# W_down of two sequences in one pass of seven block products

## The chip, the cores and the metric

The kernel runs on one core of one Trainium2 chip. The metric is the device time of one execution in microseconds. Three executions of the kernel before took 2009.88, 2016.78 and 2017.57 us; their median, 2016.78, is the time before.

## The reference

One encoder layer is applied to two sequences that share their weights: a prompt of 1024 tokens and a sample of 512, both with 1024 channels, 16 meta tokens put in front. Its mixing part (attention over a neighbourhood, a Fourier branch, gates) isn't touched by the change. What matters is the end of the layer:

```
x = x + mixed @ w_out
a = relu(rmsnorm(x, g_mlp) @ w_up)          # w_up   (1024, 4096)
return x + (a * a) @ w_down                 # w_down (4096, 1024)
```

then a last RMSNorm, and the meta tokens are dropped. Everything is float32. A product of two float32 matrices is made of three matmuls in a faster 32-bit format: each operand is split into a high part (a cast on ACT) and a low part (the operand less its high part, a subtraction on DVE or POOL), and high x high, high x low and low x high are summed (`mm3`, line 116).

## The kernel before

The program is traced in Python and put in order by a planner that works from priorities; each engine and each DMA queue then runs its instructions strictly in its own order. `pinned()` and `behind(marks)` are orders written out by hand: what is traced inside comes, on its own engine, behind the instructions named. Nearly all large transfers are issued on SP's queue. A tile pool with `bufs=n` has n places; an instruction that writes a place waits until its earlier user is done.

The sample comes first, then the prompt.

**The sample's MLP** (class `Mlp`, line 1059). The 4096 hidden channels are 32 slices of 128. `up` makes one slice: the product with W_up (24 matmuls, 512 tokens wide), ReLU on ACT, the square on DVE, and the split into high and low parts, which stay in SBUF. `down` (line 1109) follows for two slices at a time: it loads two slices of W_down, splits them (ACT, then POOL), and for each of the four tiles of 128 tokens and each half of the 1024 columns adds the product onto the tile's sum `acc` on DVE. So up and down alternate, two slices each; the last `down` takes four slices. `combine` (line 1093) makes four combinations T1 to T4 of W_down's blocks on POOL while these lie in SBUF, and stores them in the DRAM tensors `wt`. Between the steps `reading` normalizes and transposes the prompt's rows for the next sequence, and `before_last` loads the prompt's four value weights. At the end the sample's sums are normalized and stored.

**The prompt's MLP** (class `Halves`, line 1161) uses the Strassen-Winograd form: a product of 2 x 2 blocks with seven block products in place of eight. W_up's outputs and their four combinations (`combinations`, line 1471) are stored as eight blocks per pair of slices in `hidden_prompt`. `down` (line 1511) runs the seven products of `DOWN` (line 1485), each a sum over eight units of four slices. A step is one product and one unit: `load` fetches a hidden block and a weight block (512 KB each; b11, b21, b22 come straight from W_down, T1 to T4 from `wt`), splits both three steps ahead, and PE multiplies 24 times, for four tiles of 128 tokens. The results stay in PSUM banks over the eight units, two sets of four banks in turn. `evict` adds a finished product to the sums or to U2 and U3, which several results share. The last product (b22) has its last three units held back and done tile by tile (`apart = 3`), so that the first tiles are normalized (`finish`, line 1543) while PE works on the others. The sums `acc` come back from DRAM during the second and third product.

Of the kernel before, what the change touches and what calls it, by code (L numbers as in the profile page):

```python
# [68 lines left out]
class Layer:  # L69
    def __init__(self, tc, ctx, ins, outs):  # L70
# [17 lines left out]
        self.wt = []  # L88
# [239 lines left out]
    def run(self, order):  # L328
# [3 lines left out]
        for i, (name, T) in enumerate(order):  # L332
# [112 lines left out]
            mlp = self.Mlp(self, hp_, mp, name, T, h2T, acc)  # L445
# [7 lines left out]
            if nxt:  # L453
# [10 lines left out]
            mlp.run(reading, before_last, gate, lambda: tile_("r1").bitcast(F32))  # L464
# [551 lines left out]
    def project_out(self, hp, p, x, T, m, wo, acc, mlp, marks):  # L1016
# [36 lines left out]
        mlp.load(2, self.pair(p, [128, 2, 512], "w", 2))  # L1053
# [5 lines left out]
    class Mlp:  # L1059
        G = 2  # L1060
        NF = FF // 128

        def __init__(self, layer, hp, p, name, T, h2T, acc):
            self.layer, self.nc, self.hp, self.p, self.name, self.T, self.h2T, self.acc = layer, layer.nc, hp, p, name, T, h2T, acc
            self.w, self.hid = {}, {}
            self.ups = [self.up(f) for f in range(self.NF)]

        def load(self, f, to=None):
            if f not in self.w:
                to = to and [x.rearrange("p a (k c) -> p (a k) c", c=128) for x in to]  # L1070
                self.w[f] = self.layer.weights(self.layer.rows("w_up", f * 128), to)

        def up(self, f):
# [4 lines left out]
            hi, lo = (t.rearrange("p a b -> p (a b)") if len(t.shape) == 3 else t  # L1078
                      for t in self.layer.pair(self.hp, [128, T] if T == 512 else [128, 2, 512], "hid", 2 * self.G))
            self.hid[f] = hi, lo  # L1080
            step = 256 if f < 3 and T == 512 else 512
            for c in range(T // step):
# [3 lines left out]
                r = self.p.tile([128, 512], F32, name="relu", bufs=2)[:, :step]  # L1086
                nc.scalar.activation(out=r, in_=ps, func=AF.Relu)  # L1087
                nc.vector.tensor_tensor(out=r, in0=r, in1=r, op=ALU.mult)  # L1088
# [4 lines left out]
        def combine(self, g, even, odd):  # L1093


            nc, wt = self.nc, self.layer.wt
            if g % 2 == 0:
                wt.append(self.layer.dram.tile([128, 2, 4, 512], F32, name=f"wt{g // 2}"))
            (b11, b12), (b21, b22) = ([x[:, i] for i in range(2)] for x in (even, odd))
            t = [self.hp.tile([128, D], F32, name="hn", bufs=2) for _ in range(2)]  # L1100
            t1, t2, t3, t4 = (x[:, i * 512:(i + 1) * 512] for x in t for i in range(2))
            to = [wt[-1][:, g % 2, 2 * i:2 * i + 2].rearrange("p a b -> p (a b)") for i in range(2)]
            for i, ops in enumerate((((t1, b12, b11), (t2, b22, t1)), ((t3, b22, b12), (t4, b21, t2)))):
                for x in ops:
                    nc.gpsimd.tensor_tensor(out=x[0], in0=x[1], in1=x[2], op=ALU.subtract)
                nc.sync.dma_start(to[i], t[i])
                yield

        def down(self, fs, last, gate):

            layer, nc, T, acc, hid = self.layer, self.nc, self.T, self.acc, self.hid
            w, raws = {}, []
            marks = layer.mark()
            for i, f in enumerate(fs):
                to = (layer.pair(self.p, [128, 2, 512], "w", 2 if T == 512 else 4) if i < 2 else
                      tuple(gate()[:, :, :512] for _ in range(2)))
                raw = self.raws[i]().rearrange("p (a b) -> p a b", a=2)
                nc.sync.dma_start(raw, layer.ins["w_down"][f * 128:(f + 1) * 128, :].rearrange("p (a b) -> p a b", a=2))
                w[f] = [t.rearrange("p a b -> p (a b)") if T == 512 else t for t in layer.split_sb(raw, *to)]
                raws.append(raw)  # L1120
            combining = chain(*(self.combine(fs[i] // 2, raws[i], raws[i + 1]) for i in range(0, len(fs), 2)))
            if last:
                for _ in combining:
                    pass
                with layer.behind(marks + layer.mark()):
                    last()
                gain = layer.gain(self.p.tile([128, D], F32, name="gain", bufs=1), "g_final")
            for t in range(T // 128):
                ts = slice(t * 128, (t + 1) * 128)
                for half in range(2):  # L1130
                    cs = slice(half * 512, (half + 1) * 512)
                    ps = layer.psum()
                    layer.mm3(ps, [(hid[f][0][:, ts], hid[f][1][:, ts], *(v[:, cs] if T == 512 else v[:, half] for v in w[f]))
                                   for f in fs])
                    with layer.tc.high_priority(offset=60) if last and t == T // 128 - 1 else nullcontext():
                        nc.vector.tensor_tensor(out=acc[t][:, cs], in0=acc[t][:, cs], in1=ps, op=ALU.add)
                with layer.pinned():
                    next(combining, None)
                if last:
                    o = self.hp.tile([128, D], F32, name="hn", bufs=2)  # L1140
                    with layer.tc.high_priority(offset=60) if t == T // 128 - 1 else nullcontext():
                        layer.norm(acc[t], gain, o, junk=self.p.tile([128, D], BF16, name="junk", bufs=1))
                    nc.sync.dma_start(layer.outs[self.name][t * 128:(t + 1) * 128, :], o)

        def run(self, reading, before_last, gate, raw):
            other = lambda: self.layer.wtile("raw", [128, D]).bitcast(F32)
            self.raws = [raw, lambda: self.p.tile([128, D], F32, name="gain", bufs=1), other, other]
            G, NF = self.G, self.NF
            for g in range(NF // G - 1):
                for f in range(g * G + (G if g else 0), (g + 2) * G):  # L1150
                    for _ in self.ups[f]:
                        pass
                next(reading, None)
                if g < NF // G - 2:
                    self.down(range(g * G, (g + 1) * G), None, gate)
            for _ in reading:
                pass
# [529 lines left out]
```

## Time and profile before

| | us |
|---|---|
| median of three executions | 2016.78 |
| the profiled execution | 2014.83 |
| its span, first to last instruction | 2013.0 |
| PE busy | 1954.8 (97%) |
| POOL busy | 958.6 (48%) |
| DVE busy | 1098.2 (55%) |
| ACT busy | 757.7 (38%) |
| share of the DMA engines on SP's and ACT's hardware queues | 47.6% |
| mean granted TensorE clock | 0.989 |

PE is the engine that does matmuls, PEld its weight loads, which run beside them. Matmuls overlap, so a matmul that is shown with 0.39 us follows its predecessor after some 0.23 us; the distance of starts is what counts. A row of the chain of waits gives the start, the length and the work that the end of the program depended on at that time. A row of the timeline gives the start, the length, the engine and line, and in brackets how long the engine had been idle before it and what ended that. A row of groups gives the number of instructions, the busy time, the mean in ns and the idle time before them; with three durations joined by slashes it gives least, median and greatest. DVE instructions of the same kind differ in length, and their starts can overlap the end of their predecessors by 0.1 us.

### The profile page before, as it was taken

The numbers are of one execution on the slowest core, as the hardware profiler recorded it, in microseconds if no ns is written. First come the engines' busy times: TensorE is split into PE (matmuls) and PEld (weight loads), VectorE is DVE, ScalarE is ACT, GpSimd is POOL, SyncE is SP. The second block draws the span as 40 slices with busy tenths as digits, with TensorE's granted clock in tenths as the row PEclk, the third lists the DMA queues.
The fourth block names the chain that finished last, engine by engine and source line by source line (L and its number), as shares of the span: only waits on it lengthen the run. The fifth ranks groups of instructions, "written<-read, shape, count | busy, mean of one in ns | idle before, by whom it ended". The sixth has DMA issues, their size and how long they took to land.

```text
span 2013.0 us, 26474 instructions
## 1 busy us (share of the span) xinstructions
PE 1954.8 (97%) x9635; PEld 1625.1 (81%) x9635; DVE 1098.2 (55%) x1916; ACT 757.7 (38%) x1325; POOL 958.6 (48%) x743
## 2 busy tenths in 40 slices
PE   6999999999999999999999999999999999999997
PEld 4887787888888878888888888887888888888886
DVE  6572445756666552566663225466666666443246
ACT  3564323433332331556552313224333333433342
POOL 3144535467776740223333223413978774644442
PEclk8999999999999999999999999999999999999999
DMA  6666773354444445455555543412444445976663
GB/s 203 170 161 200 217 228 94 96 178 157 147 156 158 150 154 200 114 139 137 135 180 174 136 118 98 160 63 85 177 168 168 172 154 193 299 236 205 194 193 122
DMA packets 275652, 326.50 MB, mean 162 GB/s; under 512 B 42872, under 2 KB 197240, under 8 KB 274968
## 3 DMA queue, kind: packets, MB, share of 16 engines
q1 hardware_dynamic: 261792, 303.92, 47.6%
q0 software_dynamic: 13728, 20.88, 4.5%
q8 instruction: 76, 1.25, 0.3%
q14 instruction: 56, 0.46, 0.1%
HBM read 235.67 MB, written 91.64 MB: 163 GB/s over the span
## 4 chain that ended last, share of the span: by engine, by line
PE 83%; DVE 6%; DMA 4%; issue 2%; ACT 2%; POOL 2%; SPq 0%; POOLq 0%; DVEq 0%; ACTq 0%
PE ps_mm L128 23%; PE ps_o L128 22%; PE ps_s L128 19%; PE ps_t L128 8%; PE ps_mm L487 2%; PE ps_mm L488 2%; PE ps_mm L489 2%; PE ps_o L629 1%; DMA w_raw<-in_w_in 1%; POOL w_lo L152 1%; PE ps_t L609 1%; DMA bm<-g_un 1%; PE ps_t L193 1%; DMA gain<-in_w_fnB 1%; DVE st L182 1%
## 5 line engine op out<-in xcount | busy, mean ns | idle before, releaser
L152 POOL TENSOR_TENSOR w_lo<-w_raw,w_hi 128x1024 fp32r<-128x1024 f32 x84 | 212.7, 2540 | 210.2 <-ACT w_hi L151 180.3
L151 ACT CAST w_hi<-w_raw 128x1024 fp32r<-128x1024 f32 x100 | 104.7, 1048 | 156.4 <-PE ps_s L128 49.9
L487 PE MATMUL ps_mm<-hT,w_hi 128*128 128x512 f32 (+3 forms) x320 | 126.5, 395 | 0.2 <-DVE k L527 0.2
L1088 DVE TENSOR_TENSOR relu<-relu 128x512 f32<-128x512 f32 (+1 forms) x35 | 63.0, 1801 | 108.0 <-ACT relu L1087 108.0
L488 PE MATMUL ps_mm<-hT,w_hi 128*128 128x512 f32 (+3 forms) x320 | 115.2, 360 | 0.0
L489 PE MATMUL ps_mm<-hT,w_lo 128*128 128x512 f32 (+3 forms) x320 | 115.2, 360 | 0.0
L603 ACT ACTIVATE sc<-sc,ast 128x288 f32<-128x288 f32 (+4 forms) x96 | 53.9, 561 | 76.5 <-DVE ast L601 76.2
L1335 POOL TENSOR_TENSOR x<-w_hi,x 128x512 fp32r<-128x512 f32 (+1 forms) x42 | 69.8, 1662 | 23.0 <-ACT x L1338 23.0
L723 POOL MEMSET bm<- 64x96 f32 (+2 forms) x64 | 11.2, 175 | 144.7 <-DVE ast L601 97.7
L152 POOL TENSOR_TENSOR w_lo<-r,w_hi 128x1024 fp32r<-128x1024 f32 x15 | 36.8, 2452 | 87.5 <-ACT w_hi L151 87.5
L629 PEld LDWEIGHTS ps_o<-pt,vb 104*64 104x64 f32 (+6 forms) x576 | 62.3, 164 | 12.2 <-POOL vb L566 4.7
L152 POOL TENSOR_TENSOR w_lo<-w_hi 128x1024 fp32r<-128x1024 f32 x18 | 45.9, 2550 | 50.0 <-ACT w_hi L151 45.8
L152 POOL TENSOR_TENSOR w_lo<-w_lo,w_hi 128x1024 fp32r<-128x1024 f32 x18 | 48.0, 2668 | 45.2 <-ACT w_hi L151 45.2
L489 PEld LDWEIGHTS ps_mm<-hT,w_lo 128*128 128x128 f32 x320 | 60.4, 189 | 8.6
L629 PE MATMUL ps_o<-pt,vb 104*64 104x128 f32 (+6 forms) x576 | 63.4, 245 | 4.0 <-POOL vb L566 2.1
L566 POOL TENSOR_TENSOR vb<-vr,vb 96x384 fp32r<-96x384 f32 (+4 forms) x48 | 48.7, 1032 | 35.6 <-ACT vb L565 30.5
L128 PE MATMUL ps_t<-gate,x 128*128 128x512 f32 x264 | 65.3, 396 | 0.0
L128 PE MATMUL ps_mm<-gate,x 128*128 128x512 f32 x256 | 64.3, 395 | 0.0
L487 PEld LDWEIGHTS ps_mm<-hT,w_hi 128*128 128x128 f32 x320 | 60.9, 190 | 2.2 <-PE ps_s L597 0.4
L488 PEld LDWEIGHTS ps_mm<-hT,w_hi 128*128 128x128 f32 x320 | 61.0, 191 | 1.7
L601 DVE CUSTOM_DVE_ANT_0 sc<-ps_s,bm 128x288 f32<-128x288 f32 (+4 forms) x96 | 46.3, 482 | 24.4 <-PE ps_s L597 13.7
L152 POOL TENSOR_TENSOR w_lo<-raw,w_hi 128x512 fp32r<-128x512 f32 x24 | 35.5, 1485 | 50.5 <-ACT w_hi L151 42.2
(664 smaller groups left out, 5872.4 us busy)
## 6 DMA issues: line engine op xcount, KB each, us to landing
w_raw<-in_w_in SPq DMA_DIRECT2D x56, 512.0 KB
w_raw<-in_w_up SPq DMA_DIRECT2D x34, 512.0 KB
wt<-hn SPq DMA_DIRECT2D x32, 512.0 KB
hidden_prompt<-h SPq DMA_DIRECT2D x32, 512.0 KB
w_hi<-hidden_prompt SPq DMA_DIRECT2D x20, 512.0 KB
w_raw<-hidden_prompt SPq DMA_DIRECT2D x18, 512.0 KB
w_lo<-hidden_prompt SPq DMA_DIRECT2D x18, 512.0 KB
w_raw<-in_w_out SPq DMA_DIRECT2D x16, 512.0 KB
```

Of the source, the lines that this page charges most:

```text
L128: self.nc.tensor.matmul(out, a, b, start=(i == 0 and not more), stop=(i == len(terms) - 1), skip_group_check=more)
L151: nc.scalar.copy(out=hi, in_=raw)
L152: (lo_engine or nc.gpsimd).tensor_tensor(out=lo, in0=raw, in1=hi.bitcast(F32), op=ALU.subtract)
L487: nc.tensor.matmul(ps, a[0], b[0], start=(kt == 0), stop=False)
L488: nc.tensor.matmul(ps, a[0], b[1], start=False, stop=False)
L489: nc.tensor.matmul(ps, a[1], b[0], start=False, stop=(kt == 7))
L566: nc.gpsimd.tensor_tensor(out=lo, in0=vs, in1=hi.bitcast(F32), op=ALU.subtract)
L601: nc.vector.tensor_tensor_reduce(out=sc[:, :W], in0=ps[:, :W], in1=bm[:, :W], scale=1.0, scalar=3e38, op0=ALU.add, op1=ALU.min, accum_out= ...
L603: nc.scalar.activation(out=sc[:, :W], in_=sc[:, :W], func=AF.Exp, bias=st[:, 0:1], scale=-1.0, accum_out=st[:, 1:2])
L629: nc.tensor.matmul(po[:m, j * 128:(j + 1) * 128], v, x, start=(i == 0), stop=(i == len(ops) - 1))
L1088: nc.vector.tensor_tensor(out=r, in0=r, in1=r, op=ALU.mult)
L1335: self.nc.gpsimd.tensor_tensor(out=to, in0=x, in1=y, op=op)
```

## The change

W_down of the sample is no longer done beside its W_up. The sample's MLP becomes a class `Up` that only makes the hidden slices. It squares them in place and stores them to DRAM as the left factors of the same seven block products, four plain blocks and four combinations made on DVE, per pair of slices. The sums of the sample after `project_out` are stored too (`sums`). Splitting the hidden slices and all loads of W_down go away from this stage, as do the four combinations on POOL and their stores; in their place `Up.combine` makes only T2, for every other unit of four slices, on POOL, and stores it (`t2`).

`Halves.down` then does W_down for both sequences: each step has six tiles instead of four, four of the prompt and two of the sample, with two tiles of `u2` and `u3` more and twelve sums. It loads a prompt block (512 KB), a sample block (256 KB) and the weight blocks. T1, T3 and T4, and T2 of the other units, are no longer loaded but made on DVE from one to four blocks of W_down and T2 (`PARTS`, `parts`) in the raw place of the first; eleven places are shared by these raw blocks, the hidden blocks have two each, and the split operands three instead of four. Products come in another order, and three of them are added on top of the one before in the same banks (`ON_TOP`). Fetch and split both run two steps ahead, the split pinned in order; some sums wait in a list (`late`) and are done one per step, the normalizations of the second half's rows among them. The last two units are held back instead of three.

```diff
-            mlp = self.Mlp(self, hp_, mp, name, T, h2T, acc)
+            self.short = mlp = self.Up(self, ap, hp_, mp, name, T, h2T)
...
-                    for q in range(4):
+                    for q in (2, 3, 0, 1):
...
                 if half:
+                    nc.sync.dma_start(mlp.sums[t], acc[t])
...
+    class Up:
...
+            self.hid = [layer.dram.tile([128, 8, 2, T // 2], F32, name=f"hidden_{name}{u}") for u in range(self.NF // 4)]
+            self.sums = [layer.dram.tile([128, D], F32, name=f"sum_{name}{t}") for t in range(T // 128)]
...
+                if f % 4 > 1 or f >= self.NF - 4:
+                    to = [x.rearrange("p a (k c) -> p (a k) c", c=128) for x in self.layer.pair(self.p, [128, 2, 512], "w", 2)]
...
-                r = self.p.tile([128, 512], F32, name="relu", bufs=2)[:, :step]
-                nc.scalar.activation(out=r, in_=ps, func=AF.Relu)
-                nc.vector.tensor_tensor(out=r, in0=r, in1=r, op=ALU.mult)
-                nc.scalar.copy(out=hi[:, cs], in_=r)
-                nc.vector.tensor_tensor(out=lo[:, cs], in0=r, in1=hi[:, cs].bitcast(F32), op=ALU.subtract)
+                nc.scalar.activation(out=r[:, cs], in_=ps, func=AF.Relu)
+                nc.vector.tensor_tensor(out=r[:, cs], in0=r[:, cs], in1=r[:, cs], op=ALU.mult)
                 yield
...
+            to = self.hid[g // 2][:, :, g % 2]
+            nc.sync.dma_start(to[:, 2 * odd:2 * odd + 2], two(r))
+            if odd:
+                (a11, a21), (a12, a22) = ([two(x)[:, i] for i in range(2)] for x in self.r.pop(g))
...
+                    nc.vector.tensor_tensor(out=k, in0=x, in1=y, op=op)
+                nc.sync.dma_start(to[:, 4:8], sums)
+
+        def combine(self):
...
+                u = g // 2
+                if u % 2:
+                    continue
...
+                nc.sync.dma_start(even, w[g * 256:g * 256 + 128, :])
+                nc.sync.dma_start(odd[:, :512], w[g * 256 + 128:g * 256 + 256, 512:])
                 yield
...
+                nc.gpsimd.tensor_tensor(out=odd[:, :512], in0=odd[:, :512], in1=even[:, 512:], op=ALU.subtract)
+                nc.gpsimd.tensor_tensor(out=odd[:, 512:], in0=odd[:, :512], in1=even[:, :512], op=ALU.add)
+                nc.sync.dma_start(layer.t2[u][:, g % 2], odd[:, 512:])
+                yield
...
-    DOWN = ((0, "b11", 0), (5, "t2", 1), (2, "b21", 0), (6, "t3", 1), (4, "t1", 0), (3, "t4", 1), (7, "b22", 0))
...
+    DOWN = ((0, "b11"), (2, "b21"), (5, "t2"), (6, "t3"), (3, "t4"), (4, "t1"), (7, "b22"))
+    ON_TOP = (1, 4, 6)
+    PARTS = dict(t1=(("b12", 1), ("b11", -1)), t2=(("b22", 1), ("b12", -1), ("b11", 1)), t3=(("b22", 1), ("b12", -1)),
+                 t4=(("b21", 1), ("b22", -1), ("b12", 1), ("b11", -1)))
+
+    def parts(self, b, u):
+
+        layer = self.layer
+        if u in layer.t2 and b in ("t2", "t4"):
+            return ([(self.w_down("b21", u), 1)] if b == "t4" else []) + [(layer.t2[u], -1 if b == "t4" else 1)]
+        return [(self.w_down(k, u), sign) for k, sign in self.PARTS.get(b, ((b, 1),))]
...
+        sources = [self.layer.short.hid[u][:, a], self.hid[u][:, :, a]] + [x for x, _ in self.parts(b, u)]
...
+            k = (self.streamed - 1) % 11
+            if k < 5:
+                return p.tile([128, 2, 512], F32R, name="raw", bufs=5)
+            return layer.wtile(("hi", "hi", "lo", "lo", "raw", "raw")[k - 5], [128, 2, 512])
+
+        def fetch(i):
+            if 1 < i < len(steps):
+                self.fetch_down(i, [lambda: p.tile([128, 2, SH], F32R, name="short", bufs=2),
+                                    lambda: p.tile([128, 2, TH], F32R, name="long", bufs=2)] + [stream] * 4)
...
+            for x, (_, sign) in zip(rest, self.parts(self.DOWN[n][1], u)[1:]):
+                nc.vector.tensor_tensor(out=rw, in0=rw, in1=x, op=ALU.add if sign > 0 else ALU.subtract)
...
+                ws, wl, ww = (layer.pair(p, [128, 2, w], k, 3) for k, w in (("hs", SH), ("h", TH), ("w", 512)))
+            got[steps[i]] = (layer.split_sb(rs, *ws, lo_engine=nc.vector), layer.split_sb(rl, *wl, lo_engine=nc.vector),
+                             layer.split_sb(rw, *ww))
...
-        apart = 3
+        apart = 2
...
-            with layer.behind(self.stored if i < 2 else []):
-                load(i + 3)
...
+            with layer.behind(self.stored if i < 6 else []):
+                fetch(i + 2)
+
+            if u < nu - 1:
                 with layer.pinned():
...
+                    load(i + 2)
...
             for t in range(nh):
-                product(banks[at][t], t, n, [u])
-            if u == nu - 1:
-                for t in range(nh):
+                product(banks[t], t, n, [u])
+                if u == nu - 1:
                     evict(n, t)
+            with layer.pinned():
+                if u == nu - 1:
+                    load(i + 2)
+                elif late:
+                    late.pop(0)()
```

More of the change, by code (lines that the diff above doesn't have):

```diff
@@ L1077, in up @@
             w = self.w.pop(f)
[L1078 to L1081, printed above, removed]
+            g, odd = divmod(f, 2)
+            if g not in self.r:
+                self.r[g] = [t.bitcast(F32) for t in self.layer.pair(self.hp, [128, T], "hid", 4)]
+            r = self.r[g][odd]
+            step = 256 if f < 3 else 512
             for c in range(T // step):
@@ L1109, in down @@
[L1109 to L1136, printed above, removed]
@@ new lines, in run @@
+        def run(self, reading, before_last):
+            layer = self.layer
+            combining = self.combine()
+            for g in range(self.NF // 2):
+                if g == self.NF // 2 - 5:
+                    marks = layer.mark()
+                if g == self.NF // 2 - 2:
+                    for _ in reading:
+                        pass
+                    for f in range(2 * g, 2 * g + 2):
+                        self.load(f)
+                    with layer.behind(marks):
+                        before_last()
+                for f in range(2 * g, 2 * g + 2):
+                    for _ in self.ups[f]:
+                        pass
@@ L1137, in down @@
                 with layer.pinned():
                     next(combining, None)
[L1139 to L1157, printed above, removed]
-            self.down(range(NF - 2 * G, NF), before_last, gate)
+                if g:
+                    next(reading, None)
```

155 lines of the change are left out of this document (86 added, 69 removed).

## The prediction

> **What bounds the kernel now.** I read the page's shares first, then the chain of waits over the two stretches that the change touches, then the timeline at their edges, and last the windows for what DVE, POOL and DMA have left there.
>
> ```profile
> span 2013.0 us, 26474 instructions
> PE 1954.8 (97%) x9635; PEld 1625.1 (81%) x9635; DVE 1098.2 (55%) x1916; ACT 757.7 (38%) x1325; POOL 958.6 (48%) x743
> PEclk8999999999999999999999999999999999999999
> DMA  6666773354444445455555543412444445976663
> PE 83%; DVE 6%; DMA 4%; issue 2%; ACT 2%; POOL 2%; SPq 0%; POOLq 0%; DVEq 0%; ACTq 0%
> ```
>
> PE is busy nearly everywhere at the full granted clock, and the chain is mostly PE. So the first term is the number of matmuls, and the second is every place where PE would have to wait. The sample's MLP in the chain of waits (start, length, what):
>
> ```profile
> 390.64 5.53 PE ps_s L128 x24
> ...
> 429.87 5.58 PE ps_o L128 x24
> 435.45 5.52 PE ps_mm L128 x24
> 440.97 0.87 PE ps_t L193 x8
> ...
> 443.23 1.36 PE ps_o L128 x6
> ...
> 710.37 5.45 POOL w_lo L152 x2
> 715.83 2.83 POOL gate L152
> 718.70 0.79 PE ps_s L128
> ...
> 741.47 3.69 PE ps_mm L128 x16
> ```
>
> A slice of W_up is 24 matmuls in 5.55 us; then six matmuls of W_down per 1.36 us, back to back, plus eight transposes (0.87 us) of a prompt tile. Only at the end does PE wait, for POOL's splits of the last four slices of W_down. Row 741.47 is already the prompt's value projection. The prompt's W_down, chain of waits and then PE's timeline:
>
> ```profile
> 1703.31 5.75 DMA w_hi<-hidden_prompt
> ...
> 1711.53 2.42 POOL w_lo L152
> ...
> 1716.77 2.72 PE ps_s L128 x12
> ```
> ```profile
> 1696.90 1.09 PE L128 MATMUL ps_mm<-x,x 128*128 128x512 f32 x4
> ...
> 1985.89 0.39 PE L128 MATMUL ps_mm<-w_hi,h_hi 128*128 128x512 f32 x1
> ...
> 2000.85 1.52 PE L128 MATMUL ps_s<-w_hi,h_lo 128*128 128x512 f32 x6
> ```
>
> Twelve matmuls take 2.72 us, 0.2267 us each, without a gap from 1696.9 to 2002.4 (1344 x 0.2267 = 304.6). Here only the matmul count sets the time.
>
> **The matmuls.** Before, W_down of the sample is 32 slices x 4 tiles x 2 halves x 3 terms = 768 matmuls, and the prompt's is 7 products x 8 units x 4 tiles x 2 x 3 = 1344. After, 7 x 8 x 6 x 2 x 3 = 2016. In the sample's stage, from 390.64 (slice 3) there remain 29 slices x 5.55 + 9 transposed tiles x 0.87 = 168.8 us, so W_up ends at 559.4 where the stage ended at 741.5: **-182.1**. The 768 matmuls are 174.1 of it; the other 8 are the stall at 712 to 725. The one pass adds 672 x 0.2267 = **+152.3**. Net -29.8.
>
> **The tail.** Before, the last three units of b22 are held back (`apart`), 18 matmuls per tile for four tiles; now two units, 12 per tile for six: both 72 matmuls, 16.3 us, so this stretch starts as far before PE's end as before. But behind each product is a normalization, now six. DVE's timeline of the four:
>
> ```profile
> 1990.17 0.69 DVE L1540 TENSOR_TENSOR acc<-acc,ps_mm 128x512 f32<-128x512 f32 x1 [7.67 <-PE ps_mm L128]
> 1992.08 0.15 DVE L174 TENSOR_SCALAR st<-st 128x1 f32<-128x1 f32 x1 [1.22 <-ACT junk L173]
> ...
> 1995.19 0.68 DVE L1540 TENSOR_TENSOR acc<-acc,ps_mm 128x512 f32<-128x512 f32 x1
> ...
> 2004.02 0.68 DVE L1540 TENSOR_TENSOR acc<-acc,ps_s 128x512 f32<-128x512 f32 x1
> ...
> 2007.88 1.28 DVE L183 SCALAR_TENSOR_TENSOR out<-acc,st,gain 128x1024 f32<-128x1024 f32 x1
> ```
>
> One costs (2004.02 - 1990.17)/3 = 4.62 us, the last 5.14; PE gives a tile each 2.72, so DVE sets the end. From the start of the stretch: 2.9 to the first sum, 5 x 4.62 + 5.14 = 31.1, against 2009.16 - 1985.89 = 23.3 before: **+7.8**. If the order lets the next sum fill the wait for ACT (1.22), it is 5 x 1.22 less, about +2. The 3.8 us after the last DVE row (to 2013.0) stay.
>
> **What feeds PE.** Durations and rates for the rest, from the groups, the timeline and the windows (columns there: length, busy PE, PEld, DVE, ACT, POOL, clock, DMA share, GB/s):
>
> ```profile
> L152 DVE TENSOR_TENSOR h_lo<-w_raw,h_hi x18: 1212/1225/2859, 1702.7 to 1975.8; 128x1024 fp32r<-128x1024 f32 x18
> 1786.96 2.99 DVE L152 TENSOR_TENSOR h_lo<-w_lo,h_hi 128x1024 fp32r<-128x1024 f32 x1
> 1785.76 0.68 DVE L1540 TENSOR_TENSOR acc<-acc,u 128x512 f32<-128x512 f32 x1
> L152 POOL TENSOR_TENSOR w_lo<-w_lo,w_hi 128x1024 fp32r<-128x1024 f32 x16 | 42.7, 2671 | 41.1 <-ACT w_hi L151 41.1
> L151 ACT CAST w_hi<-w_raw 128x1024 fp32r<-128x1024 f32 x16 | 16.8, 1048 | 1.4 <-DMA w_raw<-wt 1.1 <-DMA w_raw<-in_w_down 0.3
> L1087 ACT ACTIVATE relu<-ps_s x12: 384/599/602, 374.4 to 684.8; 128x512 f32<-128x512 f32 x10, 128x256 f32<-128x256 f32 x2
> L1088 DVE TENSOR_TENSOR relu<-relu x35: 405/1264/2786, 377.3 to 712.9; 128x512 f32<-128x512 f32 x29, 128x256 f32<-128x256 f32 x6
> 704.63 1.31 POOL L1105 TENSOR_TENSOR hn<-w_raw 128x512 f32<-128x512 f32 x1 [1.26 <-issue]
> ```
> ```profile
> 407.08:613.00 205.92, 205.92 (x937) 169.26 (x937) 132.85 (x206) 75.31 (x107) 142.58 (x72) 1.00 0.49 160
> 712.00:725.00 13.00, 8.70 (x26) 5.56 (x25) 3.45 (x3) 2.51 (x4) 10.44 (x5) 0.74 0.43 132
> 1716.00:1756.00 40.00, 40.00 (x178) 33.15 (x177) 18.07 (x9) 19.47 (x21) 26.40 (x10) 1.00 0.92 297
> 1756.00:1796.00 40.00, 40.00 (x178) 33.11 (x178) 17.76 (x17) 14.77 (x15) 18.50 (x8) 1.00 0.74 240
> ```
>
> *W_up of the sample, alone.* Per pair of slices (11.1 us): POOL 2 x 2.5 for low parts and, for every other pair of pairs, 2 x 1.31 for T2; ACT 2 x (1.05 + 0.6); DVE two squares (1.26) and four sums of 256 columns (0.41), about 4. All fit. DMA: 1 MB of W_up, 1 MB of stores (hidden and sums), 1 MB of T2 traffic for even units, 0.5 MB of prompt rows in nine of the pairs: 2.6 to 3.7 MB, 236 to 331 GB/s where 297 was carried at a share of 0.92. Four pairs of split places let W_up run slices ahead, and the average (283) is under what was carried, so I take 0; an average pair at 240 GB/s (the 0.74 window) would be 2 us late each. The stores go through SP's queue; a W_up load behind a store waits for DVE's squares, which the same places cover. At the end the slices from 28 have two split places instead of four, and four value weights share POOL and DVE with them: **+2**, between 0 and the 8 of today's stall. T2's two instructions use acc0 and acc1, free there because the sums lie in DRAM.
>
> *Start of the pass.* Units 2 and later are fetched behind W_up's last store (1703.3). PE needs unit 2 at 1696.9 + 2 x 8.16 = 1713.3; landing 5.75 later, then three ACT casts (0.6 + 1.05 + 1.05) and POOL's 2.42 give 1714.2: **+1** (0 to 4).
>
> *Steady steps.* A step is 36 matmuls, 8.16 us (before 5.44). It casts 2.7 us on ACT and splits 0.69 + 1.23 on DVE and 2.5 on POOL. Combinations are DVE instructions of 1.23: one for T1 and T3, two for T2 in odd units and none in even ones, three for T4 in odd units and one in even ones. With one late sum (0.68) T4 costs DVE 6.3 in odd and 3.8 in even units. DVE is slowed when POOL works beside it: 2.99 and 2.86 in place of 1.23.
>
> The Trainium skill (SBUF - State Buffer, "SBUF: two separate sides") says that a DVE operation with two SBUF inputs and a GpSimd operation hold a shared port pair exclusively. The row of 2.99 agrees: 1.23 and most of a POOL instruction. By the row alone T4 fits (6.3 of 8.16); by the rule its odd units take 6.3 + 2.5 = 8.8 and the even ones 6.3, 0.6 us late per odd unit if nothing were made ahead, 2.6 in all.
>
> *At a change of product* the evictions go first on DVE, then the load of the next unit 1: 0.7 + 3 x 1.23 + 1.05 + 2.5 = 7.9 of 8.16 for T4, less for others: **+1** over six changes (0 to 5). Banks: eight, six in use, each evicted within five tiles' products (6.8 us).
>
> *The raw places.* The hidden blocks have two places, so the fetch of a step starts only when DVE has split the step two earlier, and what the SP queue holds behind it (the sums, the weights) waits too. An odd T4 step brings 0.26 + 0.52 + 4 x 0.52 = 2.9 MB, an even one 1.8: 4.7 per 16.3 us, 289 GB/s. T2 with the sums of six tiles asks the same. In T4 the odd cycle is 5.6 on DVE + 0.5 issue + 2 to start (of the 3.8 us behind the last DVE row a 0.5 MB store at 297 takes 1.8) + 2.9 MB at 297 = 9.7, 17.8 in place of 16.3, the first time eaten by the lead of one step. Three repeats at 1.5 and as much in a softer T2: **+6**, with 0 if the lead covers it and 34 as in the first rival.
>
> **Sum.** -29.8 + 7.8 + 2 + 1 + 1 + 6 = -12.0. The profiled execution took 2014.83 (its span 2013.0 and 1.8 around it), 0.1% under the median of 2016.78: **2003 us**.
>
> **Rivals.**
> *DMA turns (slower).* In the eight odd units of T2 and T4 fetch and combination follow each other instead of overlapping. For it: the two places and a demand of 289 where the profile carried 297. If the even fetch lies ahead in the same rings and a POOL instruction falls on the combinations, the pair lasts 5.6 + 2.2 + 0.5 + 2 + 9.7 + 0.5 = 20.5, 4.2 over, eight times 34: 2014.8 - 29.8 + 7.8 + 4 + 34 = 2031. It ends above before once a pair takes 16.3 + 18/8 = 18.6 us. Against it: eleven weight places, and two steps of 16.3 us less 2.7 on ACT and 2.5 on POOL leave 11 us between a landed block and its use.
> *DVE and POOL in each other's way (no change).* If most DVE instructions cost 2 or more, T4 and the changes lose 17 us: 2014.8 - 29.8 + 7.8 + 4 + 17 = 2014. For it the 2.99; against it POOL's 2.5 of 8.16.
> *All hidden.* Only matmuls and the short tail: 2014.8 - 29.8 + 2 = 1987.
> *W_up starves (the freed matmuls become waiting).* 14 pairs 2 us late: 2003 + 28 = 2031. Against: the lead.
>
> The Trainium skill (TensorE: Matmul & The Clock Gate, "What's actually happening") says PE falls to half clock after an idle window of about 3.4 us. The clock of 0.74 at 712 agrees: 4.3 us of gaps, 3 more of slow matmuls. By it gaps of 1 to 2 us between full steps cost only themselves, and a longer one two or three more.
>
> **How the numbers follow.** Forecast (1995 to 2010) 0.45, all hidden 0.20, no change 0.16, DMA turns 0.14, starving 0.05. 0.5% is about what a measurement of this kernel tells from no change: from 2006.7 to 2026.9. Faster: 0.20 and 0.38 of the forecast's 0.45, 0.58. Same: 0.07 + 0.16 + a little of the slow cases 0.04, 0.27. Slower: 0.15. Range: 1986 (all hidden) to 2026, which leaves out the slow rivals and a little below; the forecast's own range is 1995 to 2010.
>
> **What would show it.** The sample's last W_up product near 559 and the pass's first matmul near 1515 to 1519. In the pass 1.36 us per six matmuls without gaps outside T2 and T4; gaps in odd units behind DMA confirm the raw places, behind DVE the port. A stretch of about 31 us from the last group of products to DVE's last instruction confirms the tail. I am wrong if PE waits in W_up, or if the pass lasts over 480 us.

## The result

The changed kernel took **1998.8 us** (median of four runs, 1996.85 to 2002.0), the kernel before 2015.4 (four runs, 2009.9 to 2017.6): ratio **0.9929**, 95% interval 0.9918 to 0.9941. It is 0.7% faster; the forecast was 2003. (Ratios here are those on record, which can differ by about 0.001 from the ratio of the medians beside them.) The profiled execution took 1999.03 us with a span of 1997.3, against 2014.83 and 2013.0.

The page of the changed kernel (span, busy time of the engines, granted clock, chain of waits by engine):

```profile
span 1997.3 us, 26425 instructions
PE 1929.5 (97%) x9539; PEld 1607.2 (80%) x9539; DVE 1160.7 (58%) x1939; ACT 739.6 (37%) x1316; POOL 813.8 (41%) x663
...
PEclk9999999999999999999999999999999999999998
...
PE 77%; DVE 8%; DMA 5%; issue 4%; POOL 2%; ACT 2%; SPq 1%; POOLq 0%; DVEq 0%; ACTq 0%
```

PE's busy time fell by 25 us and the span by 15.7, so some of what the removed matmuls freed was turned into waiting. DMA's share of the chain rose. PE's timeline at the end of the sample's W_up shows where:

```profile
542.11 1.98 PE L128 MATMUL ps_mm<-gate,w_lo 128*128 128x512 f32 x8
550.26 0.80 PE L128 MATMUL ps_mm<-w_hi,hT 128*128 128x512 f32 x1 [6.18 <-ACT w_hi L151]
552.69 0.79 PE L128 MATMUL ps_mm<-w_lo,hT 128*128 128x512 f32 x1 [1.63 <-POOL w_lo L152]
553.28 0.63 PE L128 MATMUL ps_mm<-w_hi,hT 128*128 128x512 f32 x1
553.71 0.63 PE L128 MATMUL ps_mm<-w_lo,hT 128*128 128x512 f32 x1
...
559.14 3.81 PE L128 MATMUL ps_s<-gate,w_hi 128*128 128x512 f32 x16
...
568.23 1.98 PE L128 MATMUL ps_o<-gate,w_lo 128*128 128x512 f32 x8
570.04 1.09 PE L128 MATMUL ps_mm<-w_hi,hT 128*128 128x512 f32 x4
```

W_up runs without a gap up to 544. Then the planner has put the first product of the prompt's value projection (`w_hi,hT`, 24 matmuls) ahead of the last two slices. PE waits 6.18 and 1.63 us for its weights, and the next matmuls come 0.43 us apart instead of 0.23. W_up's last product ends at 570.21. Less the 5.55 us of that value product this is 564.7, where the forecast's sum would have given 556.6 (slice 3 starts at 387.8 here, 2.8 us earlier than before, and 168.8 us follow): **8.1 us late**. The chain of waits over the gap:

```profile
530.36 4.05 DMA w_raw<-in_w_in
...
536.07 2.48 DVE hid_lo L1096
...
538.57 2.51 DVE hn L1107
...
542.43 0.50 SPq L1126
...
543.03 6.11 DMA w_raw<-in_w_in
...
549.17 1.05 ACT w_hi L151
...
550.29 2.36 POOL w_lo L152
```

The value weights (`in_w_in`) use the two raw places of the W_up blocks, and in SP's queue their load stands behind stores of squares and sums (`hid_lo`, `hn`) that DVE made in 2.5 us each beside POOL, where they take 0.69 and 0.42 alone. The pass itself, on PE's timeline (first matmul, the only two waits, last matmuls), and the two instructions of POOL that the waits ended with:

```profile
1521.23 1.09 PE L128 MATMUL ps_mm<-x,y 128*128 128x512 f32 x4
...
1540.04 0.80 PE L128 MATMUL ps_mm<-w_lo,h_hi 128*128 128x512 f32 x1 [1.93 <-POOL w_lo L152]
...
1796.03 0.50 PE L128 MATMUL ps_t<-w_lo,h_hi 128*128 128x512 f32 x1 [1.17 <-POOL w_lo L152]
...
1982.71 1.07 PE L128 MATMUL ps_o<-w_hi,hs_lo 128*128 128x512 f32 x4
```
```profile
1537.64 2.35 POOL L152 TENSOR_TENSOR w_lo<-raw,w_hi 128x1024 fp32r<-128x1024 f32 x1 [16.41 <-ACT w_hi L151]
...
1793.59 2.38 POOL L152 TENSOR_TENSOR w_lo<-raw,w_hi 128x1024 fp32r<-128x1024 f32 x1 [19.77 <-ACT w_hi L151]
```

From 1521.2 to 1983.8 are 462.6 us for 2016 matmuls, which take 457.0 at 0.2267: 5.6 us over, no gap in the steps with T2 or T4 but at the change to T4. And DVE's timeline at the end:

```profile
1955.70 3.41 DVE L152 TENSOR_TENSOR h_lo<-long,h_hi 128x1024 fp32r<-128x1024 f32 x1
...
1964.12 3.42 DVE L152 TENSOR_TENSOR h_lo<-long,h_hi 128x1024 fp32r<-128x1024 f32 x1
...
1972.53 0.68 DVE L1566 TENSOR_TENSOR x<-x,ps_s 128x512 f32<-128x512 f32 x1
...
1992.33 1.28 DVE L183 SCALAR_TENSOR_TENSOR out<-x,st,gain 128x1024 f32<-128x1024 f32 x1
```

The last stretch (two units for each of six tiles) starts with its first matmul at 1967.3, and DVE ends at 1993.6: 26.3 us, against 23.3 before. From PE's end to the end of the span are 13.5 us, against 10.6.

| place | before to after, us | forecast |
|---|---|---|
| matmuls | -29.8 | -29.8 |
| stages ahead of slice 3 | -2.8 | 0 |
| end of W_up | +8.1 | +2 |
| from there to the pass | +1.1 | 0 |
| pass beyond its matmuls (4.8 more than before) | +4.8 | +8 |
| tail | +2.9 | +7.8 |
| sum | -15.7 | -12.0 |

### The profile page after: what moved, and what is told of

It reads as the page before. It is cut to its first block, busy times and chain, and to the rows that moved or that the text cites. A ratio compares the mean times of both kernels' runs of the same rounds, so it can differ in the third digit from the quotient of the medians.

```text
span 1997.3 us, 26425 instructions
## 1 busy us (share of the span) xinstructions
PE 1929.5 (97%) x9539; PEld 1607.2 (80%) x9539; DVE 1160.7 (58%) x1939; ACT 739.6 (37%) x1316; POOL 813.8 (41%) x663
## 3 DMA queue, kind: packets, MB, share of 16 engines
q8 instruction: 75, 1.23, 0.3%
## 4 chain that ended last, share of the span: by engine, by line
PE 77%; DVE 8%; DMA 5%; issue 4%; POOL 2%; ACT 2%; SPq 1%; POOLq 0%; DVEq 0%; ACTq 0%
PE ps_mm L128 21%; PE ps_o L128 20%; PE ps_s L128 17%; PE ps_t L128 10%; PE ps_mm L487 2%; PE ps_mm L488 2%; PE ps_mm L489 2%; DMA w_raw<-in_w_in 1%; POOL w_lo L152 1%; PE ps_o L629 1%; DVE st L181 1%; DVE h_lo L152 1%; DMA gain<-in_w_fnB 1%; PE ps_t L609 1%; PE ps_t L193 1%
## 5 line engine op out<-in xcount | busy, mean ns | idle before, releaser
L152 POOL TENSOR_TENSOR w_lo<-w_raw,w_hi 128x1024 fp32r<-128x1024 f32 x76 | 193.2, 2545 | 251.8 <-ACT w_hi L151 202.6
L152 POOL TENSOR_TENSOR w_lo<-raw,w_hi 128x1024 fp32r<-128x1024 f32 (+1 forms) x49 | 100.9, 2063 | 214.3 <-ACT w_hi L151 205.3
L151 ACT CAST w_hi<-w_raw 128x1024 fp32r<-128x1024 f32 x92 | 96.4, 1049 | 179.3 <-PE ps_s L128 53.1
L152 DVE TENSOR_TENSOR h_lo<-long,h_hi 128x1024 fp32r<-128x1024 f32 x54 | 84.7, 1571 | 79.1 <-ACT h_hi L151 79.1
L151 ACT CAST h_hi<-long 128x1024 fp32r<-128x1024 f32 x54 | 56.7, 1050 | 107.0 <-issue 34.9
L152 DVE TENSOR_TENSOR hs_lo<-short,hs_hi 128x512 fp32r<-128x512 f32 x54 | 63.8, 1182 | 41.7 <-ACT hs_hi L151 39.6
L151 ACT CAST w_hi<-raw 128x1024 fp32r<-128x1024 f32 (+1 forms) x49 | 40.9, 839 | 94.3 <-DVE raw L1541 51.1
L601 DVE CUSTOM_DVE_ANT_0 sc<-ps_s,bm 128x288 f32<-128x288 f32 (+4 forms) x96 | 46.3, 482 | 25.0 <-PE ps_s L597 10.8
```

What stands on the lines that cost most here:

```text
L151: nc.scalar.copy(out=hi, in_=raw)
L152: (lo_engine or nc.gpsimd).tensor_tensor(out=lo, in0=raw, in1=hi.bitcast(F32), op=ALU.subtract)
L601: nc.vector.tensor_tensor_reduce(out=sc[:, :W], in0=ps[:, :W], in1=bm[:, :W], scale=1.0, scalar=3e38, op0=ALU.add, op1=ALU.min, accum_out= ...
```

## The experiments

All are edits of the changed kernel; each ratio is to the kernel before, on the same chip. To read the W_up stage I take from its first product (`ps_s<-gate,w_hi`, 366.50 in the changed kernel) to the first product of the prompt's queries and keys (`hT,k`, 609.86 there). In the five profiled kernels in which nothing of this stage differs (the changed one, e4, e7, e11 and e12) this is 243.4, 246.0, 244.4, 243.2 and 243.5 us, so less than 3 us there is not told apart by one profile.

### The end of W_up: the places, or PE's order

```diff
e1_own_places
-  self.wv[q] = self.value_weights(q, ...)
+  raw = ap.tile([128, D], F32, name=f"acc{2 + q % 2}").rearrange("p (a b) -> p a b", a=2)
+  self.nc.sync.dma_start(raw, self.ins["w_in"][...])
+  self.wv[q] = self.split_sb(raw, *to, lo_engine=...)
e2_order_only
-  self.project_v(name, T, hT, att, self.wv)
+  with self.behind(self.mark((mybir.EngineType.PE,))):
+      self.project_v(name, T, hT, att, self.wv)
```

> The four value weights of the prompt are loaded into acc2 and acc3, which lie idle in this stage, instead of the two raw places that the W_up blocks use; everything else as changed. Theory A (the last W_up blocks are late because their raw places and the queue of stores are shared with the value weights): the gaps of 6.18 and 1.63 us at 544 to 553 and the slow matmuls behind them go, W_up's last product ends near 560 in place of 570, and the time falls by 7 to 10 us, to about 1989 to 1992. Theory B (PE's order alone, a value product ahead of the last two slices, is what waits): the value weights come no earlier than the splits on ACT and POOL allow, a gap of 4 us or more stays before the first value product, and the time falls by less than 4 us.

> The value products of the prompt are held behind everything that PE was given before them, so that the last two slices of W_up come first on PE; loads, places and splits stay as changed. Theory A (loads late): PE waits as long as before, now for the last W_up blocks and then for the value weights; the time changes by less than 3 us. Theory B (PE's order alone): the gap of 6.18 us shrinks to 2 or less, since slices 30 and 31 fill it, and the time falls by 6 to 9 us.

**e2** gave 0.9964 (0.9951 to 0.9977), worse than the changed kernel by 0.35%; the stage took 249.7, 6.3 more, where theory A had less than 3 us either way. PE's timeline:

```profile
561.71 6.29 PE L128 MATMUL ps_s<-gate,w_hi 128*128 128x512 f32 x16 [12.89 <-ACT w_hi L151]
```

The same wait, longer, is now on slice 30: the last W_up blocks were no earlier than the value weights. PE's order is not the cause; theory B falls.

**e1** gave 0.9928 (0.9912 to 0.9943), no gain; its six runs lie at 1992 (two, the profiled one among them) and 1999 to 2001 (four). In the profile the value weights are ready in time, and another wait has come up. PE's and POOL's timelines:

```profile
544.80 3.78 PE L128 MATMUL ps_mm<-gate,w_lo 128*128 128x512 f32 x8 [4.05 <-POOL w_lo L152]
```
```profile
539.82 1.28 POOL L1128 TENSOR_TENSOR acc<-acc,acc 128x512 f32<-128x512 f32 x1 [8.66 <-DMA acc<-in_w_down]
541.18 1.26 POOL L1129 TENSOR_TENSOR acc<-acc,acc 128x512 f32<-128x512 f32 x1
542.40 5.18 POOL L152 TENSOR_TENSOR w_lo<-w_raw,w_hi 128x1024 fp32r<-128x1024 f32 x2
```

POOL works in order: T2's two instructions waited 8.66 us for their W_down blocks, loads that in SP's queue stood behind late stores, and the low parts of W_up slices 28 and 29 waited behind T2. That is neither theory as written: shared places are one cause, T2's work at the end of the stage is a second, and taking one away brings up the other.

### T2 for other units, and the stores in another queue

```diff
e5_t2_units_135
-                if u % 2:
+                if u % 2 == 0 or u == 7:
e6_stores_act_queue
-            nc.sync.dma_start(to[:, 2 * odd:2 * odd + 2], two(r))
+            nc.scalar.dma_start(to[:, 2 * odd:2 * odd + 2], two(r))
...
-                nc.sync.dma_start(to[:, 4:8], sums)
+                nc.scalar.dma_start(to[:, 4:8], sums)
```

> T2 is made ahead for units 1, 3 and 5 instead of 0, 2, 4 and 6: the first late unit of each product (unit 1) then needs no long combination, and the last quarter of W_up carries no T2 work. Theory cover (the 1.17 us wait at the change to T4 is the three combinations of unit 1 behind the evictions): that wait goes, 1 to 2 us. Theory queue (the loads of the last W_up blocks stand in one queue behind stores and T2 loads): W_up ends 3 to 5 us earlier, measured from its first product. Both: 3 to 7 us less than the changed kernel, about 1992 to 1996 where that one takes 1999. If the raw places decide at the end of W_up, it ends as late as before and only the 1 to 2 us are won.

> The stores of the sample's hidden values and of their sums are issued from ACT's queue instead of SP's; nothing else moves. Theory queue (a W_up load waits behind a store, which waits for a DVE square that POOL slows): the last W_up blocks land earlier, the wait of 6.18 us at the end of W_up falls to 2 or less, the time by 4 to 8 us. Theory places (two raw places shared with the value weights): the wait stays at 4 us or more and the time within 3 us. Against both: ACT's casts now wait behind the stores, and PE could wait in the middle of W_up, which showed no gap before.

**e5**: 0.9919 (0.9904 to 0.9934), not told apart from the changed kernel. W_up took 242.3, within the scatter, with 4.9 us of waits left at its end; the value weights still share the places. The wait at the change to T4 is gone, as theory cover said, and the pass took 459.4 instead of 462.6.

**e6**: 0.9975 (0.9966 to 0.9984), worse. The waits at the end of W_up shrank from 7.8 to 3.3 us, so the queue had its part in them, but the stage took 251.5, 8.2 more: PE now waited at seven transposes of prompt rows before. PE's timeline:

```profile
421.88 1.94 PE L193 MATMUL ps_t<-ident,r 128*128 128x128 f32 x8 [2.82 <-DVE r L183]
...
461.92 1.06 PE L193 MATMUL ps_t<-ident,r 128*128 128x128 f32 x8 [1.52 <-DVE r L183]
...
561.54 0.49 PE L128 MATMUL ps_mm<-w_lo,hT 128*128 128x512 f32 x1 [1.77 <-POOL w_lo L152]
```

The normalization that makes `r` needs ACT too. That ACT stood at a store is the likely reason; no run shows it by itself.

### What feeds the pass

```diff
e3_no_t2_ahead
-                if u % 2:
-                    continue
+                continue
e4_no_combinations
-        return [(self.w_down(k, u), sign) for k, sign in self.PARTS.get(b, ((b, 1),))]
+        return [(self.w_down(k, u), sign) for k, sign in self.PARTS.get(b, ((b, 1),))][:1]
e12_two_thirds_of_matmuls
         def product(ps, t, n, us):
+            if t >= nl and us[0]:
+                return
```

> T2 is made ahead for no pair: all eight units of T2 take three blocks, all eight of T4 four, so that T4 asks 2.9 MB per step of 8.16 us (353 GB/s) and DVE 6.3 us per step; the T2 work leaves the W_up stage. If DMA is what the forecast's charge of 6 us and the slower rival stand for, the pass now shows gaps behind DMA: 8 steps of T4 at about 1.7 us over each, 10 to 18 us in T4, some in T2, and the time goes up by 8 to 20 us. If the lead covers the odd units with room to spare (what the changed kernel's gapless odd steps suggest), the loss is under 6 us. The W_up stage may win 1 to 3 us by its lighter DMA traffic.

> The pass leaves out the combinations of W_down: each of T1 to T4 is made from its first block alone (T2 from memory where it was made ahead for T2's own product), so DVE does up to three instructions of 1.23 us less per unit and the extra blocks are not fetched; the layer computed is another one. If the combinations are hidden as the forecast has it, only the 1.17 us gap at the change to T4 and some of the start of the pass go: 0 to 2 us. If combination and DMA of the odd units cost the pass something that the gaps do not show (slower matmuls, evictions late), the time falls by more than 5 us.

> The pass leaves out the products of the sample's two tiles in seven of its eight units (588 matmuls, 133 us at 0.2267), so that a step needs 5.44 us of PE in place of 8.16, while everything that feeds it stays; the sample's rows are then not the layer's. It shows what the feed alone takes. If a pair of odd and even T4 steps is as heavy as the slower rival had it (20.5 us per pair), the pass shortens by under 100 us, with long waits in T2 and T4. If the lead hides 17.8 per pair at most, T4's four pairs (16.3 with all matmuls, 10.9 without) lose about 7 us each and T2's about 4, and the time falls by 80 to 110. If the feed has room everywhere, by nearly 133.

**e3**: 0.9939 (0.9926 to 0.9952). The pass took 467.3 us, 4.7 more, and the W_up stage 240.0, 3.4 less. All of the loss in the pass lies at its start (waits of 0.69 and 1.93) and at the change to T4 (2.13, and slow matmuls behind it). The steady steps, 2.9 MB each in T4, were covered, but by the lead: POOL's low parts of T4's units 2 and 7 lie 42.9 us apart, 8.58 per unit against PE's 8.16, so that the feed falls back 2.1 us over five units. Windows over the end of T2 with most of T3 and over T4, then the two low parts (columns of the windows: length, busy PE, PEld, DVE, ACT, POOL, clock, DMA share, GB/s):

```profile
1700.00:1765.00 65.00, 65.00 (x289) 53.81 (x288) 47.33 (x41) 22.15 (x25) 24.29 (x9) 1.00 0.91 327
...
1800.00:1832.00 32.00, 32.00 (x141) 26.47 (x140) 31.56 (x25) 8.79 (x11) 10.90 (x4) 0.99 0.90 309
```
```profile
1799.84 2.77 POOL L152 TENSOR_TENSOR w_lo<-w_lo,w_hi 128x1024 fp32r<-128x1024 f32 x1 [2.91 <-ACT w_hi L151]
...
1842.74 2.41 POOL L152 TENSOR_TENSOR w_lo<-w_hi 128x1024 fp32r<-128x1024 f32 x1 [6.93 <-ACT w_hi L151]
```

**e4**: 0.9923 (0.9908 to 0.9938). Without combinations the wait at T4 is gone and the pass took 461.3, 1.3 us less: about all they cost.

**e12**: 0.9561 (0.9541 to 0.9580, two runs); the time fell by about 75 us, less than any case of the expectation but the slower rival's. The total misled, though: it had been worked out as if only T2 and T4 could bind, and steps of T3 and T1 took 7.0 and 6.4 us and those of the last product 9.0, where the matmuls left need 5.44. The pace of T4 itself is told by POOL's low parts of an odd, an even and the next odd unit, and a window over T2 tells what DMA carried there:

```profile
1743.98 2.38 POOL L152 TENSOR_TENSOR w_lo<-raw,w_hi 128x1024 fp32r<-128x1024 f32 x1 [7.17 <-ACT w_hi L151]
1751.00 2.38 POOL L152 TENSOR_TENSOR w_lo<-raw,w_hi 128x1024 fp32r<-128x1024 f32 x1 [4.63 <-ACT w_hi L151]
1760.54 2.38 POOL L152 TENSOR_TENSOR w_lo<-w_lo,w_hi 128x1024 fp32r<-128x1024 f32 x1 [7.17 <-ACT w_hi L151]
```
```profile
1610.00:1660.00 50.00, 50.00 (x222) 41.38 (x222) 43.03 (x32) 19.94 (x24) 19.75 (x8) 1.00 0.99 367
```

An odd and an even step of T4 take 1760.54 - 1743.98 = 16.56 us by the feed alone, 0.24 more than PE's 16.32; over four pairs that is 1 us, which a lead of one step covers. The slower rival had 20.5, the forecast 17.8. DMA moved 367 GB/s at a share of 0.99, so the 297 of the page before was not its limit.

### DVE and POOL in the pass

```diff
e7_weights_first
+            w = layer.split_sb(rw, *ww, lo_engine=nc.vector if n == len(self.DOWN) - 1 else None)
             got[steps[i]] = (layer.split_sb(rs, ...), layer.split_sb(rl, ...),
-                             layer.split_sb(rw, *ww))
+                             w)
...
+        order = list(range(2, len(sources))) + [0, 1]
e11_no_pool
-                             layer.split_sb(rw, *ww))
+                             layer.split_sb(rw, *ww, lo_engine=nc.vector))
```

> Two edits in the pass, told apart by their places in the trace. (1) In each step the weight block is fetched and split ahead of the two hidden blocks: the wait of 1.93 us at the start of the pass and the half-speed matmuls behind it go, 2 to 3 us, if the order in the queue and not the first DMA's latency sets it. (2) In the last product the low parts of the weights are made on DVE instead of POOL, so that the low parts of the hidden blocks no longer take 3.4 us beside POOL: DVE's work per step falls from 8.4 to about 7.5 us, and DVE reaches the last stretch free. If what DVE had not finished by then sets the tail, the tail of 13.6 us (last matmul to the end) falls by 1 to 3; if the six normalizations alone set it, it stays.

> The changed kernel with the low parts of all weights of the pass on DVE, none on POOL, so that DVE and POOL are never in each other's way there; DVE does one instruction of 1.23 us more per step. Theory port (POOL's splits cost DVE, and the other way round, more than they save): h_lo takes 1.22 us throughout, the wait at T4 shrinks and the tail falls by 2 to 3 us; 2 to 5 us less. Theory room (DVE is full in T4: 6.3 + 1.23 = 7.5 of 8.16 us in odd steps): waits behind DVE in odd units of T4 or at its start of 2 us and more, and no gain.

**e7**: 0.9955 (0.9942 to 0.9968), worse. The wait at the start of the pass fell from 1.93 to 0.41 and the tail from 13.5 to 10.8, both as hoped, but the change to T4 cost 8.96 us. PE's, POOL's and the end of DVE's timeline there:

```profile
1799.41 0.79 PE L128 MATMUL ps_t<-w_lo,h_hi 128*128 128x512 f32 x1 [8.96 <-POOL w_lo L152]
```
```profile
1789.15 10.21 POOL L152 TENSOR_TENSOR w_lo<-raw,w_hi 128x1024 fp32r<-128x1024 f32 x1 [19.75 <-ACT w_hi L151]
```
```profile
1794.19 1.22 DVE L152 TENSOR_TENSOR h_lo<-long,h_hi 128x1024 fp32r<-128x1024 f32 x1
1795.33 1.22 DVE L1542 TENSOR_TENSOR raw<-raw 128x1024 f32<-128x1024 f32 x1
1796.46 0.69 DVE L1567 TENSOR_TENSOR x<-x,u 128x512 f32<-128x512 f32 x1
```

POOL's instruction, 2.4 us alone, took 10.21. DVE ran instructions with two operands in SBUF back to back from 1782.7 to 1797.2, all at their undisturbed 1.22 (0.69 for half the width), and POOL ended 2.2 us after the last of them. That DVE kept POOL out is read from these times; in e9, where the order is another, POOL's low parts at this change take 2.8 and the wait is gone.

**e11**: 0.9901 (0.9886 to 0.9915), 1992.2 us. With no POOL in the pass, `h_lo` takes 1.22 throughout, both waits of the pass are gone (458.1 us) and the tail is 10.8. The 1.23 us more per step found room: theory room falls. It doesn't follow that collisions of DVE and POOL cost the pass 4.5 us: at both waits of the changed kernel POOL's low part took 2.35 and 2.38, as alone, and part of the gain is that DVE does the same in 1.22. The summary of `h_lo` (min, median and max in ns) and DVE's last row:

```profile
L152 DVE TENSOR_TENSOR h_lo<-long,h_hi x54: 1212/1224/1227, 1533.6 to 1956.5; 128x1024 fp32r<-128x1024 f32 x54
```
```profile
1983.75 1.28 DVE L183 SCALAR_TENSOR_TENSOR out<-x,st,gain 128x1024 f32<-128x1024 f32 x1
```

The last stretch's first matmul is at 1961.5 and DVE ends at 1985.0: 23.6 us with six normalizations, about as long as with four before (23.3).

### Together

```diff
e8_all_four: e1 + e5 + e7
e9_places_t2_first: e1 + e5 + e7's low parts on DVE, weights first only in the first product:
+        pairs = list(zip(raws, sources))
+        for raw, src in pairs if n else pairs[::-1]:
e10_t2_unit_1: as e9, with
-                if u % 2:
+                if u != 1:
```

> Own places for the value weights, T2 for units 1, 3 and 5, weights first in the pass, low parts of the last product on DVE, all in one kernel. If the losses found are separate waits, their gains add: 5 at the end of W_up, 2 at the start of the pass, 1 at T4, 1 to 2 in the tail, about 9 us under the changed kernel, 1988 to 1991. If they hide each other, less than 5.

> As e8 (own places for the value weights, T2 for units 1, 3 and 5, the last product's low parts on DVE), but the weight block goes first only in the first product. In e7 and e8 the order with the weights first made DVE run combinations and splits without a break at the change to T4 and POOL's low part beside them took 10.21 and 6.27 us, where it takes 2.4 alone. If that is the cause of the waits of 8.96 and 1.94 us at T4, they are gone here and the time is 2 to 4 us under e8's, about 1981 to 1983. If the fetch order has nothing to do with it, a wait of 1 us or more stays at T4. At the end of W_up PE should run without a gap again, as in e8, since both edits for it are here.

> As e9, with T2 made ahead for unit 1 alone. Steady steps of T2 and T4 then nearly all take three and four blocks (353 GB/s asked in T4), but the first step after a change of product is light. Theory changes-only (combinations and transfers cost something only where the product changes): no wait in T2 or T4 beyond 0.5 us, the time within 2 us of e9 or better, since W_up carries 2 MB less. Theory transfers (T4 cannot be fed at that rate): waits behind DMA or the combinations late in T4, 5 us or more over e9.

**e8**: 0.9861 (0.9844 to 0.9878). W_up took 234.4 us, 9.0 less than the changed kernel, where the two edits alone showed 3.3 and 1.1, and no wait is left at its end: the two causes hid each other. At T4 1.94 us were still lost behind a POOL instruction of 6.27.

**e9**: **0.9844** (0.9828 to 0.9860), 1979.9 us where before took 2013.2: the best here. W_up 234.2, pass 458.2 without a wait at T4, tail 10.9. Its interval overlaps e8's, so that the order matters is told by the wait that is gone, not by the time. **e10**: 0.9849 (0.9833 to 0.9865), the same within the intervals; W_up 232.7, pass 458.0. Its windows over the end of T2 with most of T3, over the change to T4 and over T4, with T2 ahead for one unit of eight:

```profile
1700.00:1765.00 65.00, 65.00 (x288) 53.85 (x287) 46.71 (x38) 20.90 (x24) 21.95 (x8) 1.00 0.73 247
1765.00:1800.00 35.00, 35.00 (x156) 28.96 (x155) 28.65 (x25) 8.18 (x10) 8.30 (x3) 1.00 0.55 182
1800.00:1832.00 32.00, 32.00 (x143) 26.50 (x142) 30.04 (x24) 12.24 (x15) 12.93 (x5) 1.00 0.86 294
```

PE is busy in every microsecond of them. POOL's low parts of T4's units 2 and 7 start at 1786.90 and 1826.24, 7.87 us per unit, so here heavy steps in a row keep up with PE. Making T2 ahead pays only for the first unit after a change of product.

## Why the prediction was right, and where only in sum

The time was right to 0.2% and the sign too, but in part because errors cancelled: the terms beside the matmuls were forecast at 17.8 us and came to 16.9, less 2.8 from earlier stages that the sum did not hold. Those 2.8 are luck: the first product of W_up starts anywhere between 362.8 and 369.7 us in the profiles of the changed kernel and its edits, none of which touches what lies ahead of it.

- **The matmuls** (-182.1 and +152.3) were right: slices of 5.55, six matmuls per 1.36 us, the pass's count. The pass began at 1521.2, two us past the forecast's 1519, by the end of W_up.
- **W_up of the sample, alone**: "0" for its length held, no wait before 544. **At the end +2** was the term most wrong, with 8.1. The step counted split places and engines' work and took the old stall as upper bound. It left out that value weights and W_up share two raw places and SP's queue, in which they stand behind stores of DVE's results, and that POOL takes T2 in its order. e1, e5 and e8 show both causes: waits of 4.1 and 4.9 us are left with one of them taken away, none with both.
- **Start of the pass +1** and **change of product +1**: the places and the engine were right. The waits are 1.93 and 1.17 us, and the start cost about 1.7 more in slow matmuls. e11 shows that POOL's low part is in both. For T4 the sum of 7.9 us came to 9.45 (from DVE's last eviction at 1786.52 to the end of POOL's low part at 1795.97), since DVE also does two low parts of hidden blocks (0.69 and 1.22) between the combinations.
- **The raw places +6** was a mechanism that does not bind. Odd steps cost PE nothing (e3, e10). Two sizes were off: a pair's cycle of 17.8 is 16.56 (e12), and 297 GB/s was taken as a limit where 327 to 367 were carried. With it falls the rival of DMA turns, and W_up did not starve either.
- **The tail +7.8** measured +2.9. The sum took 4.62 us per tile from a row that held a wait for ACT (1.22) and a chain that the planner can lay across two tiles; the low bound of 2 named that. And e11 shows that six normalizations need hardly more than four did (23.6 and 23.3): the 2.9 is DVE arriving late. With `h_lo` of 3.4 us beside POOL a step of the last product takes 8.42 on DVE (1955.70 to 1964.12) where PE needs 8.16; e7, with POOL out of this product alone, has the short tail too.
- **DVE and POOL in each other's way**, the rival priced at 17 us for DVE: the mechanism is there and costs 2.8 us in the tail (e7, e11). In the pass all of POOL's work costs 4.5 against doing it on DVE (e11), collisions and POOL's longer instruction together, so the 17 did not come. And in e7 it was POOL that waited, which the rival did not have.

The Trainium skill (SBUF — State Buffer, "Who interferes with whom") says that whichever of the two starts first gets the shared pair for its whole instruction and the other blocks until then. The rows agree that DVE's 1.22 becomes 3.4 where POOL began first (at 1955.04, DVE at 1955.70). POOL's 10.21 us goes further: it was kept out while eight DVE instructions began and ended, not one.

## What to carry to other kernels

At the end of a stage, ask for each queue, raw place and in-order engine who stands in front of the last block, since two causes that wait side by side show little when removed one at a time (3.3 and 1.1 us alone, 9.0 together). A rate that a profile shows at less than full DMA share need not be a limit (297 GB/s at 0.92, 367 at 0.99), and a duration with a wait inside is no cost. Where DVE runs without a break, work beside it on POOL is not free: moving it onto DVE, which had room and does it in half the time, won 0.3% here.

## What the runs showed of the hardware that was not expected

POOL can be kept out by DVE for a long time: 10.21 us for an instruction of 2.4, while DVE's own instructions beside it kept their 1.22 (e7); 6.27 in e8.

A wait of 1.93 us was enough to lower the granted clock, but not always. Windows behind the same wait at the start of the pass, in the changed kernel and in e6 (wait 1.94):

```profile
1540.00:1544.00 4.00, 3.96 (x10) 3.17 (x11) 3.85 (x3) 2.65 (x4) 2.56 (x1) 0.57 0.96 342
```
```profile
1546.60:1550.60 4.00, 3.93 (x17) 3.29 (x18) 4.00 (x3) 1.65 (x3) 3.14 (x2) 1.00 0.92 310
```

Ten matmuls against seventeen in 4 us. Other profiles fall on both sides too: after 1.93 us in e4 the clock was 0.59 (1542.6 to 1546.6), after 1.89 in e5 it was 1.00 (1540 to 1544). The prediction had taken from the Trainium skill (TensorE: Matmul & The Clock Gate, "What's actually happening") that an idle window of about 3.4 us lowers the clock, and had worked out by it that gaps of 1 to 2 us cost only themselves; this row differs, and the measurement decides. The same section calls the window free-running, so that the same wait could fall on either side of it; no run here varies that alone.

What stays open is how often each wait at the end of W_up decides from run to run: e1's runs lie 8 us apart in two groups, and only one of each kernel was profiled.
